# The scores of heads 4 to 7 ahead of the values of heads 0 to 3

## The chip, the cores and the metric

The kernel runs on one core of one Trainium2 chip. Its time is the device time of one execution in microseconds (us); what is compared is the median of several executions. Inside the core five engines work side by side, each through its own queue: TensorE (PE in the profile; its weight loads are PEld) multiplies matrices and writes to the accumulators in PSUM, VectorE (DVE) and ScalarE (ACT) work element by element, GpSimd (POOL) does a few small things, and SyncE (SP) starts the transfers (DMA) that bring the weights from memory. The engines wait for each other by semaphores.

## The reference

Two layers of a decoder over 256 tokens of width 1024, all in float32. A layer is a feed-forward block, a mixer and another feed-forward block. The mixer is what matters here:

```
z = rms_norm(x) @ w_in              # pooling input u, q, k, v (512 each), gate logits (2 x 1024)
y_pool = pooled(u)                  # trailing means over 2/4/8/16 tokens minus the token, a map per group
q, k   = rope(rms_norm(q)), rope(rms_norm(k))       # per head: 8 heads of 64
p      = softmax(q k^T / 8, causal)                 # per head, 256 x 256
y_attn = p v
gates  = sigmoid(gate logits + b)
x     += (gates[0] * (y_pool @ w_pool) + gates[1] * (y_attn @ w_attn)) @ w_out
```

The sequence is one attention block long, so the selection of earlier blocks in the reference selects nothing, and attention is plain causal attention.

## The kernel before

**Numbers.** Weights and activations are split into a high part and a rest (`split`, lines 103 and 104; `halves`, lines 179 and 180), and a product is summed from matmuls of these parts (type float32r). So each block of weights (1 MB) is loaded by SP, its high parts are written by ScalarE (L103) and its rests by VectorE (L104), and then TensorE reads it. `unit()` hands out the next block and keeps two ahead; there are four buffers for raw blocks and six half-block buffers for split ones.

**The mixer.** `mix` first computes q, k, v and u, then the gates. The gate logits take eight calls of `gate(f)`, each a chain of 32 matmuls into one large PSUM buffer (a "gate" below), drained by ScalarE (L175) and VectorE (L176). All the attention is strung between these gates, so that the gates' matmuls run while the other engines work on the softmax. Attention goes by pairs of heads, p = 0 to 3 (heads 2p and 2p + 1):

- `scores(qT, kT, p, fq)`: four matmuls (L446) into one PSUM tile per head ("sc"), and behind them the softmax of each head on VectorE and ScalarE: masked maximum (L457, two per head), exponentials (L462, two per head) into an SBUF tile "pr", and normalisation (L466).
- `by_key(pr)`: three transposes on TensorE per head (L472) into a PSUM tile "pt", copied by ScalarE (L474) to an SBUF tile "pT".
- `heads_end(ps)`: for each pair of `ps` the products of probabilities and v (`values`, L481) into one PSUM tile "y", and then the split of y into two parts (`halves`, L179 on ScalarE, L180 on VectorE) for the later branch product.

The order around the change is: gate 0, scores of pairs 0 and 1, gates 1 and 2, transposes of pairs 0 and 1, gate 3, then the **values of pairs 0 and 1, then the scores of pairs 2 and 3**, gates 4 and 5, the map of the pooled groups (tile "yp"), gate 6, transposes of pairs 2 and 3, gate 7, values of pairs 2 and 3, and the branch products (tile "pt" of line 118).

**Who sets the order.** TensorE runs in the order of the program, as the kernel asks for by

```
ctx.enter_context(tc.manual_schedule(engines={mybir.EngineType.PE}))
```

On the other engines a planner of the framework sets the order when the kernel is built: of what is ready it takes what stands first in the program, by its own estimate of durations. It also hands out the buffers, and a buffer is free again when everything that reads its last tile is done.

**Buffers.** Large PSUM buffers ("mm", two): the gates, and by way of exception the scores of head 4. Small ones ("at", four): the other scores, "pt", "y", "yp". SBUF tiles "pr" and "pT" share five buffers ("t512") with a few others.

Of the kernel before, what the change touches and what calls it, by code (L numbers as in the profile page):

```python
# [40 lines left out]
def trunk_kernel(ctx: ExitStack, tc: tile.TileContext, x_in, w_in, pw_in, qkn_in, rope_in, mask_in, band_in, out):  # L41
# [60 lines left out]
    def split(w, hi, lo):  # L102
        a = act(hi, w, AF.Copy)  # L103
        last_split[:] = [a.ins, tt(lo, w, hi.bitcast(F32), op=OP.subtract).ins]  # L104
# [73 lines left out]
    def halves(d, v):  # L178
        act(d[:, 0, :], v, AF.Copy)  # L179
        tt(d[:, 1, :], v, d[:, 0, :].bitcast(F32), op=OP.subtract)  # L180
# [259 lines left out]
    def scores(qT, kT, p, fq, scs=None):  # L440

        scs = scs or [pat.tile([P, 3 * P], F32, name="sc", tag="at") for _ in range(2)]
        for c, qs, ks in ((slice(0, S), slice(P, S), slice(0, S)), (slice(S, 3 * P), slice(0, P), slice(0, P))):
            for s, sc in enumerate(scs):
                hs = slice(s * DH, (s + 1) * DH)
                mm(sc[:, c], lhsT=qT[hs, p, qs], rhs=kT[hs, p, ks], start=True, stop=True)  # L446
        return [softmax(sc, fq[:, :, 2 * p + s]) for s, sc in enumerate(scs)]

    def softmax(sc, f):

        nb = small.tile([P, 2], F32, name="nb", tag="nb")
        su = small.tile([P, 2], F32, name="su", tag="su")
        cols = (slice(0, S), slice(S, 3 * P))
        mk3 = mask.rearrange("p a b -> p (a b)")
        for j in range(2):

            nc.vector.tensor_tensor_reduce(sc[:, cols[j]], sc[:, cols[j]], mk3[:, cols[j]], 1.0, 4 * NEG,  # L457
                                           op0=OP.add, op1=OP.max, accum_out=nb[:, j:j + 1])
        stt(nb, nb, -1.0, f, op0=OP.mult, op1=OP.mult)
        pr = tmp.tile([P, 3 * P], F32, name="pr", tag="t512", bufs=5)  # L460
        for j in range(2):
            act(pr[:, cols[j]], sc[:, cols[j]], AF.Exp, scale=f[:, j:j + 1], bias=nb[:, j:j + 1],  # L462
                accum_out=su[:, j:j + 1])
        nc.vector.reciprocal(su, su)
        for j in range(2):
            di = nc.vector.tensor_scalar(pr[:, cols[j]], pr[:, cols[j]], su[:, j:j + 1], None, op0=OP.mult)  # L466
        return pr, di.ins
# [9 lines left out]
    def values(pTs, v, p, y):  # L477
        for t in range(2):
            for s, pT in enumerate(pTs):
                h = 2 * p + s  # L480
                mm(y[s * DH:(s + 1) * DH, t * P:], lhsT=v[:, t, h * DH:(h + 1) * DH],  # L481
                   rhs=pT[:, :S] if t == 0 else pT[:, S:], start=t == 0, stop=t == 1)

    def pool_weights(l):
        raw = raws.tile([P, 2 * HALF], F32, name="raw", tag="raw")
        hl = parts.tile([P, 2, HALF], F32R, name="hl", tag="hl")
        nc.sync.dma_start(raw[:, :GW], pw_in[l])
        split(raw[:, :GW], hl[:, 0, :GW], hl[:, 1, :GW])
        return [hl]
# [30 lines left out]
    def mix(l, after, cs):  # L520
# [12 lines left out]
        def gate(f):  # L533
            return pair(unit(), gates[:, f])

        def heads_end(ps):

            y = pat.tile([P, len(ps), S], F32, name="y", tag="at")
            for i, p in enumerate(ps):
                values(pTs.pop(p), v, p, y[:, i, :])  # L540
            for i, p in enumerate(ps):
                halves(yk[p], y[:, i, :])
# [38 lines left out]
        for p in (0, 1):  # L581
            pTs[p] = [by_key(pr) for pr, _ in prs[p]]
        gate(3)
        heads_end((0, 1))

        sc = pmm.tile([P, 3 * P], F32, name="sc", tag="mm")
        prs[2] = scores(qT, kT, 2, fq, [sc, pat.tile([P, 3 * P], F32, name="sc", tag="at")])
        prs[3] = scores(qT, kT, 3, fq)
        pw = pool_weights(l)
        gate(4)  # L590
        gate(5)
# [98 lines left out]
    for l in range(L):  # L690
        cs = []
        ffn(lambda f: prep(f, l, C_GM), NK if l else NK + 1, None if l else ah, mid=lambda: cs.extend(turns(l)))
        mix(l, lambda f: prep(f, l, C_G2), cs)
        if l + 1 < L:
            ffn(lambda f: prep(f, l + 1, C_G1), NK + 1)
        else:
            ffn(lambda f: nc.sync.dma_start(out[:, f, :], x[:, f, :]), NK + 1, last=True)
# [90 lines left out]
```

## Time and profile before

| | |
|---|---|
| median of 3 runs | 1001.1 us (1000.55 to 1001.76) |
| profiled execution | 1003.4 us |
| its span, first to last instruction | 1001.3 us |
| TensorE busy, its weight loads | 995.8 us (99%), 896.5 us (90%) |
| VectorE busy | 797.9 us (80%) |
| ScalarE busy | 634.4 us (63%) |
| GpSimd busy | 17.9 us (2%) |
| read from memory | 190.89 MB, 192 GB/s over the span |
| granted TensorE clock | 1.00 |

A row of the timeline or of the chain gives the start of a piece and its duration in us, the engine, the line of the program (L446) and the tile it writes ("sc"), and "x16" the number of instructions in it. "out<-in" names the tile written and those read. In brackets stands how long the engine was idle ahead of it and what ended the idle time. One `mm` of the program on plain float32 operands appears as two matmuls with a weight load each: the 8 calls for four heads are 16 rows. A group's row gives the busy time in us and the mean of one instruction in ns.

### The profile page before, as it was taken

What the parts mean: (1) busy time and instruction counts of PE and PEld (TensorE: products, weight loads), DVE (VectorE), ACT (ScalarE), POOL (GpSimd) and SP (SyncE); (2) the same over time, 40 slices, a digit from 0 to 9 for tenths busy, and PEclk for the clock granted to TensorE, in tenths of its full rate; (3) what the DMA queues carried; (4) which work ended last, traced back from release to release, by engine and by line L of the source; (5) the groups of instructions that cost most, each with busy time, mean ns of one, the idle gap of its engine ahead of it and who ended that gap; (6) DMA issues with size and microseconds to landing.
All of it is one profiled execution on the core that took longest, in us unless ns stands there. A gap on an engine that the chain in (4) does not pass through costs nothing.

```text
span 1001.3 us, 15710 instructions
## 1 busy us (share of the span) xinstructions
PE 995.8 (99%) x6148; PEld 896.5 (90%) x6148; DVE 797.9 (80%) x1313; ACT 634.4 (63%) x1013; POOL 17.9 (2%) x40
## 2 busy tenths in 40 slices
PE   9999999999999999999999999999999999999998
PEld 8888888889899889988889988888889988888897
DVE  7887777798978987776787777778987899888752
ACT  7866655657776766665576666556676777666541
POOL 0000000001000100000000000000000001000000
PEclk9999999999999999999999999999999999999999
DMA  8765655554545665655555565564536456655640
GB/s 301 267 233 192 212 207 193 175 179 138 215 164 174 210 215 200 211 184 200 206 184 200 206 201 184 205 210 169 180 114 228 165 199 210 206 189 207 211 147 22
DMA packets 30601, 192.94 MB, mean 193 GB/s; under 512 B 3392, under 2 KB 5824, under 8 KB 8000
## 3 DMA queue, kind: packets, MB, share of 16 engines
q1 hardware_dynamic: 30240, 191.69, 55.3%
q8 instruction: 48, 0.79, 0.3%
q10 hardware_dynamic: 288, 0.26, 0.1%
q14 instruction: 25, 0.20, 0.1%
HBM read 190.89 MB, written 1.05 MB: 192 GB/s over the span
## 4 chain that ended last, share of the span: by engine, by line
PE 96%; DMA 2%; DVE 1%; ACT 1%; issue 0%; SPq 0%; DVEq 0%
PE ps L118 76%; PE pt L118 9%; PE pl L118 6%; DMA raw<-w 2%; PE pe L118 2%; PE sc L446 1%; PE y L481 1%; DVE hl L104 1%; PE pt L472 1%; PE tp L437 0%; ACT hl L103 0%; PE yp L118 0%; SPq L650 0%; DVE ab L309 0%; DVE ab L176 0%
## 5 line engine op out<-in xcount | busy, mean ns | idle before, releaser
L118 PE MATMUL ps<-hx,hl 128*128 128x512 f32 (+1 forms) x3200 | 541.3, 329 | 1.0 <-DVE ab L176 1.0
L118 PEld LDWEIGHTS ps<-hx,hl 128*128 128x128 f32 x3200 | 481.2, 188 | 56.0 <-DVE ab L176 1.3
L104 DVE TENSOR_TENSOR hl<-raw,hl 128x1024 fp32r<-128x1024 f32 (+2 forms) x371 | 441.9, 1196 | 111.6 <-ACT hl L103 110.8
L103 ACT ACTIVATE hl<-raw 128x1024 fp32r<-128x1024 f32 (+2 forms) x371 | 382.5, 1034 | 132.4 <-PE ps L118 90.0
L118 PE MATMUL ps<-ga,hl 128*128 128x512 f32 (+1 forms) x1024 | 176.3, 328 | 0.0
L118 PEld LDWEIGHTS ps<-ga,hl 128*128 128x128 f32 x1024 | 153.8, 188 | 17.3
L175 ACT ACTIVATE ab<-ps 128x512 f32<-128x512 f32 x84 | 50.2, 598 | 85.9 <-PE ps L118 85.9
L176 DVE TENSOR_TENSOR ab<-ps,ab 128x512 f32<-128x512 f32 x84 | 58.0, 690 | 42.6 <-ACT ab L175 42.5
L118 PE MATMUL ps<-gb,hl 128*128 128x256 f32 (+1 forms) x390 | 69.4, 326 | 0.0
L118 PEld LDWEIGHTS ps<-gb,hl 128*128 128x128 f32 x390 | 58.0, 188 | 6.3
L311 ACT ACTIVATE sg<-ab 128x256 f32<-128x256 f32 x88 | 36.7, 419 | 34.5 <-DVE ab L309 20.9
L118 PE MATMUL pt<-ax,hl 128*128 128x256 f32 x384 | 44.5, 276 | 0.0
L118 PEld LDWEIGHTS pt<-ax,hl 128*128 128x128 f32 x384 | 44.2, 188 | 0.3 <-DVE gates L176 0.3
L118 PE MATMUL pl<-hl,hx 128*128 128x512 f32 (+1 forms) x256 | 44.1, 330 | 0.0
L118 PEld LDWEIGHTS pl<-hl,hx 128*128 128x128 f32 x256 | 38.5, 187 | 5.0
L312 DVE TENSOR_TENSOR sg<-sg,ab 128x256 f32<-128x256 f32 x88 | 36.5, 419 | 0.5 <-ACT sg L311 0.5
L343 ACT ACTIVATE t<-ps 128x256 f32<-128x256 f32 x40 | 15.2, 379 | 32.7 <-PE ps L118 32.7
L208 ACT ACTIVATE hx<-gx 128x256 fp32r<-128x256 f32 x48 | 23.9, 504 | 10.2 <-DVE gx L351 5.3
L309 DVE TENSOR_TENSOR ab<-ab,r 128x256 f32<-128x256 f32 x66 | 27.7, 423 | 1.8
L179 ACT ACTIVATE ga<-sg 128x256 fp32r<-128x256 f32 x64 | 25.6, 404 | 4.1 <-DVE sg L312 3.9
L180 DVE TENSOR_TENSOR ga<-sg,ga 128x256 fp32r<-128x256 f32 x64 | 26.5, 419 | 0.0
L209 DVE SCALAR_TENSOR_TENSOR hx<-gx,hx 128x256 fp32r<-128x256 f32 x48 | 22.8, 480 | 2.8 <-ACT hx L208 2.8
(126 smaller groups left out, 676.3 us busy)
## 6 DMA issues: line engine op xcount, KB each, us to landing
raw<-w SPq DMA_DIRECT2D x176, 1024.0 KB, 4.9
raw<-w SPq DMA_DIRECT2D x9, 256.0 KB, 5.1
raw<-w SPq DMA_DIRECT2D x2, 512.0 KB, 7.3
out_dram<-gx SPq DMA_DIRECT2D x8, 128.0 KB, 1.9
gx<-x SPq DMA_DIRECT2D x3, 256.0 KB, 4.8
raw<-w SPq DMA_DIRECT2D x4, 128.0 KB, 4.7
raw<-pw SPq DMA_DIRECT2D x2, 256.0 KB, 2.7
raw<-w ACTq DMA_DIRECT2D x2, 128.0 KB, 3.8
```

Of the source, the lines that this page charges most:

```text
L103: a = act(hi, w, AF.Copy)
L104: last_split[:] = [a.ins, tt(lo, w, hi.bitcast(F32), op=OP.subtract).ins]
L118: return mm(steps(ps), lhsT=w, rhs=steps(xk), start=first, stop=last)
L175: a = act(t, ps[:, :, 1, :], AF.Copy)
L176: return a.ins, tt(t, ps[:, :, 0, :], t, op=OP.add).ins
L179: act(d[:, 0, :], v, AF.Copy)
L180: tt(d[:, 1, :], v, d[:, 0, :].bitcast(F32), op=OP.subtract)
L208: act(hx[:, f, 0, :], x[:, f, :], AF.Copy, scale=g)
L209: stt(hx[:, f, 1, :], x[:, f, :], g, hx[:, f, 0, :].bitcast(F32), op0=OP.mult, op1=OP.subtract)
L309: tt(ab[:, 0, :], ab[:, 0, :], r, op=OP.mult)
L311: act(sg, ab[:, 0, :], AF.Silu)
L312: tt(sg, sg, ab[:, 1, :], op=OP.mult)
```

## The change

In `mix` one line moves: the values of pairs 0 and 1, with the split of their result, stand behind the scores of pairs 2 and 3. Both still stand between gate 3 and gate 4, so TensorE's order there goes from gate 3, values, scores, gate 4 to gate 3, scores, values, gate 4, in each of the two layers. No instruction is added, removed or changed in size. The second call of `heads_end`, for pairs 2 and 3, stays where it is.

```
         gate(3)
-        heads_end((0, 1))
 
         sc = pmm.tile([P, 3 * P], F32, name="sc", tag="mm")
         prs[2] = scores(qT, kT, 2, fq, [sc, pat.tile([P, 3 * P], F32, name="sc", tag="at")])
         prs[3] = scores(qT, kT, 3, fq)
+        heads_end((0, 1))
         pw = pool_weights(l)
         gate(4)
         gate(5)
```

More of the change, by code (lines that the diff above doesn't have):

```diff
@@ L583, in mix @@
         gate(3)
-        heads_end((0, 1))
         sc = pmm.tile([P, 3 * P], F32, name="sc", tag="mm")
@@ L588, in mix @@
         prs[3] = scores(qT, kT, 3, fq)
+        heads_end((0, 1))
         pw = pool_weights(l)
```

## The prediction

> **What bounds the kernel now.** I read the page of the profile first, then TensorE's own waits, then the chain of work that ended last, around the change. The page gives the busy time of the engines, and the list of TensorE's waits the only places in the whole run where it stood still for another engine (us in total, times, the longest):
>
> ```profile
> PE 995.8 (99%) x6148; PEld 896.5 (90%) x6148; DVE 797.9 (80%) x1313; ACT 634.4 (63%) x1013; POOL 17.9 (2%) x40
> ```
>
> ```profile
> core 0 of [0], span 1001.3 us
> PE busy L192 <- DVE eps L194: 1.0, 1, 1.0
> PE ps L118 <- DVE ab L176: 1.0, 1, 1.0
> ```
>
> TensorE is busy in 995.8 of 1001.3 us. Of the 5.5 us that are left, two waits of 1.0 us are named, and neither stands at a line that the change touches (L192 is the warm-up, L176 at the tile "ab" is the first feed-forward block). No wait of TensorE is left that a better order in the mixer could remove. The chain that ended last confirms it for the place of the change (start, duration, what; "ps" are the gates, "sc" the scores, "y" the values, "pt L472" the turning of the probabilities of heads 4 to 7, "yp" the pooling map); the last two rows are the same place in the second layer:
>
> ```profile
> 236.16 1.51 PE sc L446 x16
> ...
> 255.31 1.45 PE y L481 x16
> 256.76 1.51 PE sc L446 x16
> 258.27 10.96 PE ps L118 x64
> 269.24 1.38 PE yp L118 x12
> ...
> 276.00 1.31 PE pt L472 x12
> ...
> 749.35 1.45 PE y L481 x16
> 750.80 1.51 PE sc L446 x16
> ```
>
> Every piece begins where the one before it ends: 255.31 + 1.45 = 256.76, 256.76 + 1.51 = 258.27. The chain is TensorE's own queue throughout, and not the softmax.
>
> **The change on TensorE.** It moves 16 recorded matmuls with 16 weight loads (values of heads 0 to 3) behind 16 and 16 others (scores of heads 4 to 7), once in each layer, and adds and removes none. The pieces trade places: before 1.45 + 1.51 = 2.96 us, after 1.51 + 1.45 = 2.96 us. That a piece keeps its length behind another neighbour can be checked in one case: the scores take 1.51 us behind a gate (236.16) and 1.51 us behind the values (256.76). What may still change is the idle time at the seams, which the timeline of weight loads shows (start, busy time; in brackets the idle time ahead):
>
> ```profile
> 255.24 1.28 PEld L481 LDWEIGHTS y<-pT,v 128*64 128x64 f32 x16 [0.23 <-issue]
> 256.69 1.39 PEld L446 LDWEIGHTS sc<-qk 64*128 64x128 f32 x16 [0.17 <-issue]
> 258.20 0.63 PEld L118 LDWEIGHTS ps<-hx,hl 128*128 128x128 f32 x4
> ...
> 282.60 1.28 PEld L481 LDWEIGHTS y<-pT,v 128*64 128x64 f32 x16 [0.23 <-issue]
> 284.05 1.09 PEld L118 LDWEIGHTS pt<-ax,hl 128*128 128x128 f32 x9 [0.17 <-DVE gates L176]
> ```
>
> Seams before: gate to values 0.23, values to scores 0.17, scores to gate 258.20 - 256.69 - 1.39 = 0.12; together 0.52 us. Behind the values stands 0.17 whether scores (256.69) or a full-width product (284.05) follows, and ahead of the values 0.23 both times, so a seam seems to go by what leaves. Seams after: gate to scores 0.23, as ahead of the values; scores to values, which no row shows; values to gate 0.17, from the row at 284.05. For the one not shown the bounds are 0 and 0.23, the largest seam here; I take 0.12, the seam that the scores leave now. The sum is 0.23 + 0.12 + 0.17 = 0.52 us, a change of 0.00; with the bounds -0.12 to +0.11 per layer, and **-0.24 to +0.22 us** for both layers.
>
> The Trainium skill, page "TensorEngine Tiling (Array Packing)", section "Key Properties", says that a change of the tiling mode drains the engine, while a change of the tile within a mode does not. The forms in the rows (128*128, then 128*64, then 64*128, then 128*128) make three changes of mode before and three after, so by that rule the sum would be 0.0 too; were each drain as long as the longest seam shown, it would be 3 x 0.23 - 0.52 = +0.17 us a layer, +0.34 in all. The trace agrees with a stop at each change (0.23, 0.17, 0.12 us) and does not decide between equal and unequal drains.
>
> **The waits that the new order could bring on TensorE.** Four inputs and buffers are asked for at another time. The rows of VectorE and of ScalarE (start, busy time, line, operation):
>
> ```profile
> 236.83 0.69 DVE L176 TENSOR_TENSOR gates<-ps,gates 128x512 f32<-128x512 f32 x1 [0.94 <-ACT gates L175]
> 237.44 0.42 DVE L457 CUSTOM_DVE_ANT_0 sc<-sc,mask 128x256 f32<-128x256 f32 x1
> ...
> 252.28 4.09 DVE L104 TENSOR_TENSOR hl<-raw,hl 128x1024 fp32r<-128x1024 f32 x4
> 256.28 0.68 DVE L176 TENSOR_TENSOR gates<-ps,gates 128x512 f32<-128x512 f32 x1
> 256.93 1.23 DVE L104 TENSOR_TENSOR hl<-raw,hl 128x1024 fp32r<-128x1024 f32 x1
> ...
> 258.40 0.42 DVE L457 CUSTOM_DVE_ANT_0 sc<-sc,mask 128x256 f32<-128x256 f32 x1
> ...
> 264.47 0.55 DVE L466 TENSOR_SCALAR pr<-pr,su 128x256 f32<-128x256 f32 x2
> ```
>
> ```profile
> 249.89 1.24 ACT L474 ACTIVATE pT<-pt 128x384 f32<-128x384 f32 x3
> ...
> 255.35 0.60 ACT L175 ACTIVATE gates<-ps 128x512 f32<-128x512 f32 x1 [1.54 <-PE ps L118]
> ...
> 260.18 0.56 ACT L462 ACTIVATE pr<-sc,nb,ri 128x256 f32<-128x256 f32 x1 [1.27 <-DVE nb L459]
> 260.64 0.19 ACT L462 ACTIVATION_READ_ACCUMULATOR pr<-sc,nb,ri 128x1 f32 x1
> 260.74 0.45 ACT L462 ACTIVATE pr<-sc,nb,ri 128x128 f32<-128x128 f32 x1
> ```
>
> - The scores, now at 255.24, need three of the four small PSUM buffers, which the turned probabilities of heads 0 to 3 held. Those are copied out by 249.89 + 1.24 = 251.13: 4.1 us to spare. The values, now at 255.24 + 1.51 = 256.75, need the fourth and the copies themselves: 5.6 us to spare.
> - Gate 4 starts at 258.20 as before, since the sum ahead of it is the same. It needs the large PSUM buffer of gate 3, drained at 256.28 + 0.68 = 256.96: 1.24 us to spare. This is the shortest cover, and the rival below attacks it.
> - Gate 5 starts halfway through the piece at 258.27, at 258.27 + 10.96 / 2 = 263.75. It needs the large buffer that holds head 4's scores, read last by the exponential that ends at 260.74 + 0.45 = 261.19: 2.6 us to spare, and the scores come earlier, not later.
> - The probabilities are normalised by 264.47 + 0.55 = 265.02 and are turned at 276.00: 11.0 us to spare. Starting the softmax up to 1.45 us earlier makes this longer, and buys nothing.
>
> What is late instead is the split of the values into two parts, two instructions each on ScalarE and VectorE, from 1.51 us later on. The next use of their buffer is at earliest the pooling map at 269.24, and of their result the branch products after 284.05. With the values ending at 258.20 that leaves 11.0 us for work of under 2 us.
>
> No DMA is issued by the moved lines, so no queue of SP or POOL is passed. What the queues bring are the weights, and the splits of them run far ahead; this row groups VectorE's splits from the start to 256.5 us:
>
> ```profile
> L104 DVE TENSOR_TENSOR hl<-raw,hl 128x1024 fp32r<-128x1024 f32 x88 | 107.2, 1223 | 26.1 <-ACT hl L103 26.0
> ```
>
> The first three blocks of weights are split in other shapes, every later one in two such instructions, and gates 0 to 7 are blocks 41 to 48 (counting from 0). So 88 splits end with block 46, gate 5: when the changed place is reached, gates 4 and 5 are already split, and gate 6 starts only after the pooling map, at 269.24 + 1.38 = 270.62. If the earlier softmax pushes the split at 256.93 behind itself, it ends even at 265.02 + 1.23 = 266.25, 4.4 us early.
>
> **The sum.** The profiled execution took 1003.4 us, its span 1001.3, so 2.1 us lie around it; the change on the chain is 0.00 (-0.24 to +0.22), which leaves 1003.4. The median of the runs shown is 1001.1 (1000.55 to 1001.76), 2.3 us under the profiled one, and the change moves it by nothing: **1001.1 us**.
>
> **The rivals.** About 0.2%, 2.0 us, is what a measurement of this kernel can tell from no change.
>
> (1) *Slower: gate 3's drain falls behind the maxima of the softmax.* TensorE's order is written out, VectorE's is the planner's. Gate 3's drain and the first masked maxima of heads 4 and 5 now come ready close together. The row on the maxima:
>
> ```profile
> L457 DVE CUSTOM_DVE_ANT_0 sc<-sc,mask x32: 287/378/468, 237.4 to 755.0; 128x256 f32<-128x256 f32 x16, 128x128 f32<-128x128 f32 x16
> ```
>
> VectorE is free at 252.28 + 4.09 = 256.37. With all eight maxima first, the drain ends at 256.37 + 8 x 0.378 + 0.68 = 260.07, and gate 4 starts 1.87 us late, 3.7 us in both layers: 1004.8. It decides from the point where more than 258.20 - 256.37 - 0.68 = 1.15 us stands ahead of the drain, so from the fourth maximum on (four: 0.36 us a layer, 1001.8). For it speaks the thin cover. Against it: scores behind a gate are already there at 236.16, and there VectorE sat idle 0.94 us for the drain's first half, drained (236.83) and only then took the first maximum (237.44). ScalarE's half is done at 255.95, before VectorE is free. Chance of a cost over 2.0 us: 5%.
>
> (2) *The exponentials wait for the values.* Probabilities and their turned copies share five SBUF buffers. At the scores four hold copies for the values, so one is free: head 4's exponential can start, those of heads 5 to 7 must wait for the values behind them on TensorE. The values end at 258.20. The first exponential now starts 260.18 - 258.40 = 1.78 us behind the first maximum; with that maximum at 256.96 at the earliest, it comes at 258.74. The wait is then over, and the time 1001.1. Should the planner put the three heads behind other work, the 11.0 us ahead of 276.00 cover it; a delay beyond that would pass to TensorE one for one, and 1.0 us a layer of it makes 1003.1. Chance of that: 2%.
> The Trainium skill, "TensorE: Matmul & The Clock Gate", section "Architectural detail", calls ScalarE and VectorE strict first-in-first-out queues: by it a blocked exponential would hold gate 4's drain too. No row of this profile has such a block at this place; by the times above its length is nothing.
>
> (3) *Faster, beyond the noise.* All seams of this place vanish: 2 x 0.52 = 1.04 us, 1000.1. The 1.0 us wait in the first feed-forward block lies ahead of the change and stays. A gain of 2.0 us would need a third of the 2.96 us of matmuls themselves in each layer, against which stand the equal 1.51 of the scores behind two neighbours. Chance of over 2.0 us: 3%.
>
> (4) *The change does not do what it says.* It surely reorders TensorE, but the planner may leave the softmax where it was: 1001.1 as well.
>
> **How the numbers follow.** No change on the chain, in its forms (1001.1, with cases 2 and 4 where they cost nothing): 88%. Rival 1 over 2.0 us 5%, rival 2 over 2.0 us 2%, faster 3%; 2% for a shifted order of splits later in the layers, half of it on either side. So faster 4%, same 88%, slower 8%. The range starts at 1000.0, with all seams gone (1001.1 - 1.04, rounded), and goes to 1002.6: the seams' 0.22, the spread of the runs upward (1001.76 - 1001.1 = 0.66), and half a microsecond for a drain that falls partly behind (0.36 to 0.72), 1.6 at most. Rival 1 in full lies outside.
>
> **What would show it.** In the chain of the changed kernel the pieces should read scores 1.51, values 1.45, gates 10.96, end to end, and TensorE's waits should name nothing new. The scores' first weight load should show 0.23 us ahead of it, the values' between 0 and 0.23. VectorE should drain gate 3 by 257 and take the first maximum about 1.4 us earlier than 258.40; the values' split should come after it. Wrong is the forecast if gate 4 waits for VectorE's drain (rival 1), if the turning at 276.00 waits for the normalisation (rival 2), or if the two pieces together are not 2.96 us.

## The result, and the profile after

The changed kernel takes 1006.82 us (median of six runs, 1005.98 to 1008.2), the kernel before 1001.43 us (median of six, 1000.55 to 1002.58): 5.4 us more, a ratio of 1.0052 (95% interval 1.0042 to 1.0062). The profiled execution took 1006.51 us, its span is 1004.4. The forecast was no change. All ratios in this document are taken from fast executions alone and need not be the quotient of the medians beside them: the median of the changed kernel with one more matmul (below) contains one execution of 2647.04 us, its ratio does not.

TensorE does not wait more than before. The page's row of busy times, and the list of TensorE's waits in the changed kernel:

```profile
PE 999.9 (100%) x6148; PEld 899.1 (90%) x6148; DVE 797.5 (79%) x1313; ACT 634.5 (63%) x1013; POOL 18.1 (2%) x40
```

```profile
core 0 of [0], span 1004.4 us
engine line waited for: us in total, times, longest us
PE busy L192 <- DVE eps L194: 1.0, 1, 1.0
```

The same 6148 matmuls are busy for 999.9 us instead of 995.8, and the only wait left is the warm-up. At the place of the change everything went as forecast. The chain around it (start, duration, what), both layers:

```profile
252.91 1.51 PE sc L446 x16
254.41 1.45 PE y L481 x16
255.87 10.97 PE ps L118 x64
266.83 1.38 PE yp L118 x12
...
750.58 1.51 PE sc L446 x16
752.09 1.45 PE y L481 x16
753.54 10.97 PE ps L118 x64
```

The pieces are 1.51 + 1.45 = 2.96 us, with gate 4 at once behind them. The seams, from the timeline of weight loads:

```profile
252.84 1.39 PEld L446 LDWEIGHTS sc<-qk 64*128 64x128 f32 x16 [0.23 <-DVE hl L104]
254.34 1.28 PEld L481 LDWEIGHTS y<-pT,v 128*64 128x64 f32 x16
255.79 0.52 PEld L118 LDWEIGHTS ps<-hx,hl 128*128 128x128 f32 x3 [0.17 <-DVE nb L457]
```

Gate to scores 0.23, scores to values 254.34 - 252.84 - 1.39 = 0.11, values to gate 0.17: 0.51 us against 0.52 before.

So the time went elsewhere. Here are the long pieces of the chain in the kernel before; "pl" is the output product behind the mixer, "ps" behind it the feed-forward blocks, and the first row is the first feed-forward block, ahead of the change:

```profile
59.11 126.59 PE ps L118 x752
...
306.33 10.73 PE pl L118 x64
317.06 10.67 PE ps L118 x64
...
337.06 166.67 PE ps L118 x1000
...
679.73 10.89 PE pl L118 x64
...
800.37 10.73 PE pl L118 x64
...
997.84 0.02 issue
```

And in the changed kernel:

```profile
57.95 125.33 PE ps L118 x752
...
303.93 10.77 PE pl L118 x64
314.70 10.77 PE ps L118 x64
...
334.90 168.33 PE ps L118 x1000
...
680.99 10.85 PE pl L118 x64
...
801.60 10.77 PE pl L118 x64
...
1000.96 0.02 issue
```

From the first output product to the next mixer the chain took 679.73 - 306.33 = 373.40 us before and 680.99 - 303.93 = 377.06 after: 3.66 us more. From the second output product to the end it took 997.84 - 800.37 = 197.47 and 1000.96 - 801.60 = 199.36: 1.89 more. Together **5.55 us**, which is the loss, and it lies in stages that the change does not touch. No wait of TensorE appears there: 1000 matmuls of the same line and the same forms take 168.33 us instead of 166.67. The profiled execution of before had started 306.33 - 303.93 = 2.40 us later into this place, by its start and its first block, so the two spans differ by 3.1 only.

The start times of single matmuls show what the two paces are; a pace is the mean time from one start to the next, and a pair is one product of 512 columns with the one of 256 behind it. Worked out from the records, ns from start to start, at 400 us (products of 512 and 256 columns in turn, four to a period):

```
before   113 221 111 221 | 114 221 110 222      666.7 a period, 333.3 a pair
after    118 221 111 223 | 118 222 110 224      673.3 a period, 336.7 a pair
```

One interval of the four is 4 to 5 ns longer in the changed kernel, and another 2 ns. The pace holds from the output product to the next mixer, over more than 2000 matmuls. The first rows above show that neither kernel owns a pace: in the first feed-forward block the kernel before took 126.59 / 752 = 168.3 ns a matmul and the changed one 125.33 / 752 = 166.7, with the same instructions. The granted clock is 1.00 in all these stages of both traces.

And this is the passage into the output product, in the first layer ("|" stands ahead of the interval to its first matmul; left of it the 256-column branch products):

```
before   109 117 117 115 115 110 | 116 225 120 225 116 238
after    115 115 110 116 117 116 115 | 109 222 113 222 116 223
```

The branch products run in a rhythm of five, four intervals of 115 to 117 ns and one of 109 or 110. The kernel before enters the output product one matmul behind the short interval (step 1), the changed one on it (step 0). The second layer shows the same steps in both. From there on the paces differ.

### The profile page after: what moved, and what is told of

Read it like the earlier page. It is cut to its first block, busy times and chain, and to the rows that moved or that the text cites. A ratio compares the mean times of both kernels' runs of the same rounds, so it can differ in the third digit from the quotient of the medians.

```text
span 1004.4 us, 15712 instructions
## 1 busy us (share of the span) xinstructions
PE 999.9 (100%) x6148; PEld 899.1 (90%) x6148; DVE 797.5 (79%) x1313; ACT 634.5 (63%) x1013; POOL 18.1 (2%) x40
## 4 chain that ended last, share of the span: by engine, by line
PE 100%; DVE 0%; issue 0%
PE ps L118 79%; PE pt L118 9%; PE pl L118 6%; PE pe L118 2%; PE sc L446 1%; PE y L481 1%; PE pt L472 1%; PE busy L192 0%; PE tp L437 0%; PE yp L118 0%; PE st L118 0%; DVE gx L351 0%; DVE ones L188 0%; DVE eps L194 0%
```

## The experiments

Theory "pace": the two paces are states of TensorE's own stream of matmuls, and the step at which the output product begins picks one; the new order shifted the step by one. Rival "buffers": the new order places tiles elsewhere, and the addresses cost the time. Rival "others": the new order of VectorE's and ScalarE's work costs it. In the two programs as built, TensorE's instructions behind the place and the addresses they use are the same. Of the tiles at the place, those in the four small PSUM buffers (the scores of heads 5 to 7 and the values) lie in other ones of the four, so "buffers" cannot be dismissed without a run.

**One matmul more in the changed kernel, four more in the kernel before.** A branch product is computed again ahead of itself in each layer, with the same result; this is the edit for one more, and for four more it has again=4:

```
-    def chain3(ps, hl, b, xs, first=True, last=True):
+    def chain3(ps, hl, b, xs, first=True, last=True, again=0):
+        for xk in [xs[0]] * again:
+            prod(ps, blk(hl, b, 0), xk[:, 0, :], True, True)
...
-                chain3(pss[e // 2][:, e % 2, 0], us[-1], e % 2 * 8, pk)
+                chain3(pss[e // 2][:, e % 2, 0], us[-1], e % 2 * 8, pk, again=1 if f0 + e == 4 else 0)
```

> The changed kernel with one matmul more in each layer: the first branch product of the second half of the columns (tile pt, 256 columns) is computed once more ahead of itself, with the same result; the orders of all other engines stay as they are. Theory 'pace' (TensorE's stream of 512- and 256-column products has two steady paces, 333.3 and 336.7 ns a pair, and which one it takes is set by the step of the five-step rhythm of the branch products at which the output product begins): one more step brings the phase of the kernel before, so the piece of 1000 matmuls takes 166.67 us instead of 168.33, and the time is 1006.8 - 5.5 + 2 x 0.115 = 1001.5 us. Rival 'buffers' (the new order gives tiles other addresses, and these cost the time) and rival 'others' (the new order of VectorE and ScalarE costs it): neither is touched, so 168.33 us and 1006.8 + 0.2 = 1007.0 us.

> The kernel before, with the values ahead of the scores, and with the same branch product computed four times more in each layer. Theory 'pace': four steps more bring the phase that the changed kernel has, so the piece of 1000 matmuls takes 168.33 us instead of 166.67, and the time is 1001.4 + 5.5 + 8 x 0.115 = 1007.8 us, as slow as the changed kernel without its change. Rivals 'buffers' and 'others': nothing of theirs is touched, 166.67 us and 1001.4 + 0.9 = 1002.3 us.

The changed kernel with one more (its chain):

```profile
336.26 166.67 PE ps L118 x1000
```

The kernel before with four more:

```profile
336.53 168.33 PE ps L118 x1000
```

With one matmul more, the changed kernel takes 1002.28 us against 1002.52 of the kernel before on the same chip, ratio 1.0003 (0.9993 to 1.0012): the whole loss is gone, for 0.23 us of added work. With four more, the kernel before takes 1008.6, ratio 1.0067 (1.0052 to 1.0082), of which 0.92 us is the added work: without the change, it is as slow as the changed kernel. In each of the two programs as built, all addresses and the orders of the other engines are those of the kernel it was made from, so neither rival can make these two results. The start times into the output product in the first layer, as above, show the expected steps, 1 and 0:

```
changed, one more    109 117 117 116 115 109 | 116 225 120 225 116 238
before, four more    115 109 116 117 116 115 | 109 223 112 222 116 223
```

These are the passages of the kernel before and of the changed kernel, to within 1 ns.

**The split of the values alone.** TensorE keeps values ahead of scores, and only the split of the values is issued behind the scores (the helper functions of the edit are left out here):

```
-        heads_end((0, 1))
+        y01 = heads_end((0, 1), False)        # values only
...
         prs[3] = scores(qT, kT, 3, fq)
+        split_y((0, 1), y01)                  # halves(yk[p], y[:, i, :])
```

> TensorE's order of the kernel before (values, then scores), but the split of the values on ScalarE and VectorE is issued behind the softmax of heads 4 to 7, as in the changed kernel. Theory 'pace': TensorE's order alone counts, 166.67 us for the 1000 matmuls and 1001.4 us. Rival 'others': the order of the other engines counts, 168.33 us and 1006.8 us.

```profile
335.27 166.67 PE ps L118 x1000
```

1001.55 us against 1002.52, ratio 1.0 (0.9987 to 1.0013). This speaks against "others" too, but it has only a part of the changed kernel's order: on VectorE both halves of the split went behind the maxima, while ScalarE's first half stayed ahead of the exponentials, which begin at 257.76:

```profile
255.02 0.38 ACT L179 ACTIVATE ax<-y 128x256 fp32r<-128x256 f32 x1
```

So it is the two runs with repeated matmuls that exclude "others". One of the ten executions here took 1005.98 us, the others 1000.79 to 1002.5; its trace was not kept, and whether it ran at the slow pace is open.

**All five steps.** Five, three, two and four more matmuls in the changed kernel, by the same edit with other counts.

> The changed kernel with the first branch product of the second half computed five times more in each layer. Theory 'pace', if the rhythm of the branch products has five steps: five more bring the phase of the changed kernel back, so 168.33 us for the piece of 1000 matmuls in both layers and 1006.8 + 10 x 0.115 = 1008.0 us. Rival 'count' (any added matmul shifts the instruction stream and frees the pace): 166.67 us and 1006.8 - 5.5 + 1.2 = 1002.5 us.

> The same with three more: a step of the rhythm that neither kernel enters the output product with. Theory 'pace' does not say which pace it gives, but it must be one of the two, 166.67 or 168.33 us for 1000 matmuls, and the same in both layers: 1002.0 or 1007.5 us. Rival 'count': 166.67 us.

> The changed kernel with two more branch products in each layer, which enters the output product at the second step behind the short interval; not measured so far. Theory 'pace': one of the two paces, 166.67 or 168.33 us per 1000 matmuls, alike in both layers, so 1001.8 or 1007.3 us. With four more it completes the five steps: 0 slow, 1 fast, 3 slow are known.

> The same with four more, the fourth step. Theory 'pace': 166.67 or 168.33 us, alike in both layers, so 1002.2 or 1007.7 us.

Five more:

```profile
336.81 168.33 PE ps L118 x1000
```

Three more:

```profile
336.40 168.33 PE ps L118 x1000
```

Two more:

```profile
336.74 168.33 PE ps L118 x1000
```

Four more:

```profile
336.57 166.67 PE ps L118 x1000
```

| step into the output product | kernels | 1000 matmuls, us | time, us |
|---|---|---|---|
| 0 | changed; changed + 5; before + 4 | 168.33 | 1006.82; 1009.0; 1008.6 |
| 1 | before; changed + 1 | 166.67 | 1001.43; 1002.28 |
| 2 | changed + 2 | 168.33 | 1008.58 |
| 3 | changed + 3 | 168.33 | 1008.38 |
| 4 | changed + 4 | 166.67 | 1003.34 |

Five more is as slow as none, which one more was not: it is the step that counts, not that something was added, so the rival "count" (any added matmul would free the pace) is out. The times of the last three rows and of five more are of one execution each; the paces are read from their traces, in which both layers agree; they were taken on different chips, so small differences of time between rows mean nothing. In this layout two steps of five give the fast pace, three the slow one.

**Addresses by themselves.** The changed kernel with its pools laid out in the opposite order (the names of the pools, in the order in which they are opened):

```
-    raws, parts, acts, tmp; pmm, pat
+    tmp, acts, parts, raws; pat, pmm
```

> The changed kernel with its buffer pools laid out in the opposite order in SBUF and in PSUM; the orders of all engines stay as they are. Theory 'pace': addresses do not matter, 168.33 us for the 1000 matmuls and 1006.8 us. Rival 'buffers': the cost hangs on where the tiles lie and should change with them, back towards 166.67 us and 1001.4 us or to a third value.

```profile
341.00 171.67 PE ps L118 x1000
```

Here my expectation missed. It takes 1021.75 us, ratio to the kernel before 1.0186 (1.0152 to 1.022), with all orders unchanged; its four executions spread from 1016.97 to 1024.83, and the trace is of the longest. The runs with repeated matmuls have shown that addresses do not explain the change; this one shows that they can matter more than the step. Two more tell SBUF and PSUM apart:

> The changed kernel with only the two PSUM pools in the opposite order, the SBUF pools as they were. With both moved, the 1000 matmuls took 171.67 us. If the PSUM places did that: 171.67 us here and about 1021 us. If the SBUF places did it: 168.33 us and 1006.8 us.

> The changed kernel with only the four large SBUF pools in the opposite order, the PSUM pools as they were. If the SBUF places made the pace of 171.67 us: 171.67 us here and about 1021 us. If the PSUM places did it: 168.33 us and 1006.8 us.

PSUM pools alone:

```profile
335.60 168.33 PE ps L118 x1000
```

SBUF pools alone:

```profile
339.48 170.00 PE ps L118 x1000
```

1007.2 and 1017.47 us (one execution each): the places in PSUM alone show no cost, those in SBUF alone some 10.7 us over the changed kernel's 1006.82. The 1000 matmuls took 170.00 us there, neither of the two values expected, so why both together give 171.67 is open. I then moved the streamed operands against the weights, by unused columns behind x, which leaves all orders alone. Everything that lies behind x in SBUF moves with them (the gates, q, k, v and the temporary tiles too):

```
-    gx = acts.tile([P, L * NG + NK * S], F32, name="gx")
+    gx = acts.tile([P, L * NG + NK * S + 104], F32, name="gx")[:, :L * NG + NK * S]
```

> The kernel before with 416 bytes of unused space behind x, which moves the streamed operands (hx, ga, gb) against the weights (hl): the distance of their first addresses, which is 160 bytes over a multiple of 512, becomes 256 over; all orders stay. In the layouts that gave 170.00 and 171.67 us for 1000 matmuls the distance is 0. Theory 'pace' with 'the distance sets the choice of paces': another pair of paces, lower than 333.3 ns if a distance far from 0 is better, by a multiple of 3.3 ns; 990 to 1002 us. If the distance does not matter: 166.67 us and the time of the kernel before.

> The same with 160 bytes, which brings the distance to 0 with the pools in their usual order. If the distance sets the choice of paces: 170.00 or 171.67 us for 1000 matmuls and 1012 to 1021 us. If the order of the pools did it in another way: 166.67 us and the time of the kernel before.

> The kernel before with 64 bytes of unused space behind x: the distance between streamed operands and weights becomes 96 over a multiple of 512, so it stays 32 over a multiple of 64. All layouts with the distance a multiple of 64 gave 170.0 or 171.7 us for 1000 matmuls, the one with 32 over gave 166.67 or 168.33. If the remainder by 64 sets the choice of paces: 166.67 us here and the time of the kernel before, 1001.4 us. If only the distance of the kernel before is good: 170 us and 1018 us.

The rows of 104, 40 and 16 columns, in this order:

```profile
340.13 170.00 PE ps L118 x1000
```

```profile
341.67 170.00 PE ps L118 x1000
```

```profile
337.59 169.58 PE ps L118 x1000
```

1018.04 us (ratio 1.0166, 1.015 to 1.0181), 1019.72 us (one execution) and 1013.75 us (ratio 1.012, 1.0104 to 1.0137). The distance between streamed operands and weights, modulo 512 bytes, was 256, 0 and 96; it is 160 in the kernel before. None of the three is as good as 160. The guess behind the first, that a distance far from 0 is good (990 to 1002 us expected), fell, and so did the one behind the last, that a remainder of 32 by 64 is. Which addresses are good, whether it is this distance at all, and why, stays open.

**A reset of the first block.** In block 9 of the first feed-forward block stand two spare matmuls of 256 columns, whose result nobody reads. They were replaced by three plain float32 ones:

```
-                pair(unit(), ab, NK, lambda: spread(ah, pat.tile([P, S], F32, name="st", tag="at")))
+                pair(unit(), ab, NK, lambda z=pat.tile([P, P], F32, name="st", tag="at"): [mm(z, lhsT=ones, rhs=ones, start=True, stop=True) for _ in range(3)])
```

> The kernel before, in whose first feed-forward block the two spare 256-column matmuls among those of block 9 are replaced by three plain float32 matmuls of 128 columns, the form behind which gate 3 took the fast pace in both kernels. Theory 'pace': such a stop resets the phase, so the rest of the first block takes 333.3 us per 1000 pairs whatever pace it had (not a change of sides, as the spare matmuls made in every profile so far): 1.7 us less where it was slow, on average some 0.8 us less than before, 1001.6 against 1002.4 us. If a stop does not reset it: the two paces either way by chance, same time as before.

1001.89 us against 1001.34, ratio 1.0005 (0.9996 to 1.0014): no gain. In its profile the pace went from 336.7 ns a pair to 333.3 behind the stop, but one profile cannot tell a reset from a change of sides, and the times speak against the expected gain. Whether it resets anything is open. No version that was run beats both kernels; the changed kernel with one matmul more is level with the kernel before.

## Why the prediction was wrong

**The step that failed** is the one that made the sum: "the change on the chain is 0.00 (-0.24 to +0.22)". It priced the pieces and the seams at the place and took every other matmul of the run at its old duration. Its words were "What may still change is the idle time at the seams": that the matmuls behind the place keep their pace was taken without a reason, and no rival doubted it. In its place the runs showed that the same matmuls have two durations, 166.7 and 168.3 ns on average, and that the order at the place decides between them for all feed-forward work behind it: 5.55 us, 25 times the 0.22 us that stood as the upper bound of the step. The range, up to 1002.6, had no term for it.

**The trace of before had the row that warns.** In the chain quoted above the first block's 752 matmuls take 168.3 ns each and the later 1000 take 166.67, on the same line with the same forms and the clock at 1.00 throughout. I looked at waits, where a saturated engine has none, and not at the pace of one form from stage to stage. Two paces in one trace say that this stream has two states; over the some 3400 matmuls behind the two mixers, 1.67 ns are 5.7 us.

**Point by point, the rest held.** The pieces and seams did (2.96 us, 0.51 us). Rival 1, the drain of gate 3 behind the maxima, did not come. VectorE in the changed kernel:

```profile
253.88 0.68 DVE L176 TENSOR_TENSOR gates<-ps,gates 128x512 f32<-128x512 f32 x1
254.47 0.41 DVE L457 CUSTOM_DVE_ANT_0 sc<-sc,mask 128x256 f32<-128x256 f32 x1
...
260.80 0.42 DVE L180 TENSOR_TENSOR ax<-y,ax 128x256 fp32r<-128x256 f32 x1
```

It drains gate 3 first, as at gate 0. The first maximum comes 254.47 - 252.84 = 1.63 us behind the start of the place, against 258.40 - 255.24 = 3.16 before: 1.5 us earlier, forecast about 1.4, and worth nothing, as forecast. The split of the values went behind the softmax (260.80 on VectorE) and TensorE did not wait for it. Rival 2 did not come either. ScalarE's first exponential:

```profile
255.95 0.56 ACT L462 ACTIVATE pr<-sc,nb,ri 128x256 f32<-128x256 f32 x1 [1.46 <-DVE nb L459]
```

It waited for the maximum, and the values had ended at 254.41 + 1.45 = 255.86, ahead of all exponentials of heads 4 to 7. The chance of 8% for slower stood on these two rivals and on shifted splits; none of the three was the cause.

The Trainium skill, "TensorE: Matmul & The Clock Gate", section "Wait — 56ns, not 53.3ns?", gives N / 2.4 GHz and some 2.5 ns from one warm matmul to the next; an estimate from that for a pair of 512 and 256 columns is 325 ns. No stream here ran so fast, and the measurement decides: 333.3 and 336.7 ns in the layout of these kernels, 339.2 to 343.3 in the others. One number for a form was exactly what misled here.

**How the order shifts the step** is shown only in part. In the first layer, from the first moved matmul to the first of gate 4 it is 2.959 us before and 2.960 after (2.959 in both in the second layer), and start to start the two kernels agree within 1 or 2 ns through gates 4 to 6. The last interval ahead of the transposes of heads 4 to 7 is 115 ns before and 111 after (114 and 112 in the second layer); behind them gate 7 settles after two longer intervals (232 and 233 ns) at different matmuls in the two kernels; and the first branch product behind the values starts 217 or 220 ns after the one before it, from where the rhythms are one step apart. The two kernels thus leave the place at most 1 ns apart, which is the unit of these records, and are a few ns apart at the transposes and one step apart at the branch products. How the small difference grows into a step is not shown, and what in the hardware holds the phase was not found.

## What to carry to other kernels

Where TensorE is saturated (busy without a wait), divide a long stage's time by its matmuls and compare stages of the same form. If one trace shows two paces, the stream has two states, and an edit to TensorE's order may flip it, as this one did; price that flip (difference times matmuls behind the edit) beside the edit's own terms, and give it a chance. Whether a loss is of this kind is told by repeating one matmul with the same result: if one more brings the time back and a full period more does not, the edit's own work is not at fault. One more that does not help proves nothing, since neighbouring steps can share a pace: here steps 2 and 3 are both slow.

## What the runs showed of the hardware

- In the layout of these kernels the stream of 512- and 256-column products keeps a pace of 333.3 or 336.7 ns a pair for over 2000 matmuls without a wait, at a granted clock of 1.00; the branch products, of 256 columns alone, run in a rhythm of five, 573.3 ns. The periods, 666.7, 673.3 and 573.3 ns, are multiples of 6.67 ns (100, 101 and 86).
- In the first feed-forward block the two spare matmuls in block 9 changed the pace to the other one in all ten profiles that have them in this SBUF layout: 333.3 to 336.7 in four, 336.7 to 333.3 in six. Which one they found differed from kernel to kernel although the instructions up to there are the same, so the loads at the start seem to set it; no run tests that.
- Where the tiles lie in SBUF alone made the kernel before 1.2% to 1.7% slower (ratios 1.012 and 1.0166, 64 and 416 unused bytes behind x): 169.58 and 170.00 us for the same 1000 matmuls instead of 166.67. With the PSUM pools moved as well, the changed kernel went from 168.33 to 171.67 us.
